# The ends of four down projections written out again: norm scalings left to the scheduler, a second result turned one product later, two products exchanged

## The chip, the cores and the metric

The kernel runs on one core of a Trainium2 chip. The metric is the device time of one execution in microseconds (us). Five engines work side by side, each through its own queue in order: TensorE (PE in the profile, its weight loads PEld), VectorE (DVE), ScalarE (ACT), GpSimd (POOL) and SyncE (SP, which issues transfers). A tile pool hands out buffers in turn; who writes a buffer again waits until its last reader is done.

## What is computed

A trunk of two layers over 512 positions of width 1024. Each layer has a half step with a gated feed-forward, a mixer (banded and dilated attention in layer 0, neighbourhood attention in layer 1), a second half step, and a per-layer input:

```python
def swiglu(x, w_gate, w_up, w_down):
    return (jax.nn.silu(x @ w_gate) * (x @ w_up)) @ w_down
...
    for i in range(DEPTH):
        h = h + 0.5 * swiglu(rmsnorm(h, norm_ffn1[i]), ffn1_w_gate[i], ffn1_w_up[i], ffn1_w_down[i])
        hn = rmsnorm(h, norm_mix[i])
        ...
        h = h + 0.5 * swiglu(rmsnorm(h, norm_ffn2[i]), ffn2_w_gate[i], ffn2_w_up[i], ffn2_w_down[i])
        gate = jax.nn.sigmoid(rmsnorm(h, norm_ple[i]) @ w_ple_gate[i])
        h = h + gate * (p[i] @ w_ple_proj[i])
    return rmsnorm(h, norm_final)
```

The product with `w_down` (2816 x 1024) is made four times: two half steps in each of two layers. These four are the down stages of this text.

## The kernel before

Activations lie as feature chunks: `h` is eight tiles of 128 features x 512 positions (chunks 0 to 7). Every number of a product is split in two parts, `wh` (or `hi`) and `wl` (or `lo`), and a product is three matmuls (hi by hi, hi by lo, lo by hi). `split` (L154, L155) makes the parts: ScalarE copies the first (L154), VectorE subtracts it for the second (L155). Weights land in `wr` (128 x 1024) or `tmp` (128 x 512) tiles; `wh` and `wl` have four buffers each, which are handed out in the order in which the weights are split.

`down` makes the product from seven products of quarters, called "first" to "seventh", each in six steps (step 0 has one chunk of the inner dimension, the others two). A step with two chunks is twelve matmuls of 128 x 512 into two banks. The list `order` (L605 to L608) is the order of all the steps. For each, `product` issues the matmuls (L595), `after` what follows it, and `ahead` the splits for the step four places later and the loads for a step behind that. Within `down`, `put` pins an instruction: it stays in program order on its engine. What is not pinned the scheduler places.

The end of a down stage goes like this. After "sixth" 5 (the last step of "sixth"), ScalarE copies two banks (L601, `c2`), VectorE makes `u3` (L656) and takes it off `c5` (L658): `c5` is one of four results, the right half of the positions of chunks 4 to 7. After "fourth" 5 VectorE makes `c21` (L662), the right half of chunks 0 to 3, whose left half, `c11`, has been ready for long. "third" 0 to 5 give the last result, the left half of chunks 4 to 7.

The results have positions on the partitions, so TensorE turns them back: `turned` (L614) makes transposes of 128 x 128 by the identity `ident`. `second_half(m, ...)` turns two chunks into one bank of `tbank` (tag `tr`, two buffers) and VectorE adds them to `h` (L630). `first_half(m)` turns one whole chunk and VectorE adds it (L620). Behind each sum `norm_split` prepares the chunk for the next stage's products: ScalarE scales it by the norm's gain (L217), VectorE makes the lower part (L218). In the kernel before all of this is pinned:

| after | what is issued |
|---|---|
| "third" 1 | `second_half` of chunks 4 and 5, from `c5` |
| "third" 2 | `second_half` of chunks 6 and 7, from `c5` |
| "fourth" 5 | `c21` |
| "third" 3 | `first_half` of chunks 0 and 1 |
| "third" 4 | `first_half` of chunks 2 and 3 |
| "third" 5 | the left half of chunks 4 to 7 (not pinned, L689 and L690) |

The next stage's first matmuls (L179 to L181 or L785 to L787) take the chunks in the order in which they come and are set between these steps by the scheduler.

Of the kernel before, what the change touches and what calls it, by code (L numbers as in the profile page):

```python
# [56 lines left out]
class Trunk:  # L57
# [92 lines left out]
    def put(self, ins):  # L150
        return self.tc.keep_in_program_order(ins) if self.pinned else ins
# [341 lines left out]
    def down(self, w, a, sums, kept, inner, turn):  # L493

        nc, H = self.nc, T // 2
        l, r = slice(0, H), slice(H, T)
# [101 lines left out]
        def copied(p):  # L598
            out = [self.act() for _ in p]
            for o, x in zip(out, p):  # L600
                put(copy(o, x, AF.Copy))  # L601
            return out
# [2 lines left out]
        order += [("seventh", 0), ("second", 5), ("first", 5), ("fifth", 4), ("seventh", 1), ("sixth", 0), ("seventh", 2),  # L605
                  ("fifth", 5), ("sixth", 1), ("seventh", 3), ("fourth", 0), ("sixth", 2), ("seventh", 4), ("fourth", 1),
                  ("sixth", 3), ("seventh", 5), ("fourth", 2), ("sixth", 4), ("fourth", 3), ("third", 0), ("sixth", 5),
                  ("fourth", 4), ("third", 1), ("third", 2), ("fourth", 5), ("third", 3), ("third", 4), ("third", 5)]  # L608

        hs, M = [], KC // 2  # L610

        def turned(out, x, j):
            for i, y in enumerate(x):
                put(nc.tensor.transpose(out[:, i * P:(i + 1) * P], y[:, j * P:(j + 1) * P], self.ident))  # L614

        def first_half(m):
            p, h = self.tbank(), hs[m]
            turned(p[:, l], c11, m)
            turned(p[:, r], c21, m)
            put(nc.vector.scalar_tensor_tensor(h, p, 0.5, h, op0=ALU.mult, op1=ALU.add))  # L620
            self.h[m] = h
            self.norm_split(m)

        def second_half(m, x, c):
            p = self.tbank()
            for j in range(2):
                turned(p[:, j * H:(j + 1) * H], x, m - M + j)
            for j in range(2):
                h = hs[m + j]
                put(nc.vector.scalar_tensor_tensor(h[:, c], p[:, j * H:(j + 1) * H], 0.5, h[:, c], op0=ALU.mult, op1=ALU.add))  # L630
                self.h[m + j] = h
                self.norm_split(m + j, c)

        def after(kind, s):
            nonlocal rb, rc, c11, c5, c2, u3, c21
            if (kind, s) in (("first", 2), ("fifth", 1)):
                turn(range(2) if kind == "first" else range(2, 4))
                if kind == "fifth":
                    rb = [self.tbank(), self.tbank()]
            elif (kind, s) == ("first", 5):  # L640
                c11 = copied(r1)
                for o, p in zip(c11, r2):
                    put(tt(o, p, o, op=ALU.add))
                rc = [self.bank(), self.obank()]
            elif (kind, s) == ("fifth", 5):
                c5 = copied(r3)
            elif (kind, s) == ("fourth", 0) and inner:
                self.p = inner()
            elif (kind, s) == ("first", 3):
                hs.extend(self.act() for _ in range(KC))  # L650
                for m in range(KC):
                    nc.sync.dma_start(hs[m], kept[m])
            elif (kind, s) == ("sixth", 5):
                c2, u3 = copied(r1), [self.act(), self.act()]
                for i in range(2):
                    put(tt(u3[i], c2[i], rb[i], op=sub))  # L656
                for i in range(2):
                    put(tt(c5[i], c5[i], u3[i], op=sub))  # L658
            elif (kind, s) == ("fourth", 5):
                c21 = [self.act(), self.act()]  # L660
                for i in range(2):
                    put(tt(c21[i], rc[i], u3[i], op=ALU.add))  # L662
            elif kind == "third" and 0 < s < 3:
                second_half(M + 2 * s - 2, c5, r)
            elif kind == "third" and 2 < s < 5:
                first_half(2 * s - 6)
                first_half(2 * s - 5)
# [14 lines left out]
        for i, step in enumerate(order):  # L682
            product(*step)
            after(*step)
            ahead(i + LEAD + 1)
# [4 lines left out]
        for m in range(M, KC, 2):  # L690
            second_half(m, c2, l)
# [935 lines left out]
```

## Time and profile before

| | |
|---|---|
| runs | 2014.23, 2016.39, 2023.58 us (median 2016.39) |
| profiled execution | 2018.9 us, of which its span is 2017.1 us |
| TensorE busy | 1979.8 us, 98% of the span; mean granted clock 0.992 |
| VectorE busy | 1551.3 us, 77% |
| ScalarE busy | 1216.8 us, 60% |
| GpSimd busy | 335.1 us, 17% |
| transfers | 348.24 MB, mean 173 GB/s |

A group of instructions in the profile has its line of the kernel, its engine, the operation and `output<-inputs` by the names of the tiles (`mm`, `sc`, `ob`, `tr` are banks). "Idle before" is the time for which the engine stood still ahead of an instruction, with the instruction that released it. In a row by time the columns are the start, the duration, the engine, the line, the operation, the operands, and how many instructions are merged into the row. A row of stretches has for each engine the busy time and the instructions, then the clock granted to TensorE (1.00 is full speed), the share of the transfer engines and GB/s. The four down stages end near 314 to 347, 953 to 981, 1343 to 1377 and 1918 to 1948 us of the span; the text calls these ends 1 to 4.

### The profile page before, as it was taken

Reading aid. Unit: us, or ns where it says so; the run is one execution under the profiler, and the core shown is the slowest. Engines: PE = TensorE matmul, PEld = TensorE weight load, DVE = VectorE, ACT = ScalarE, POOL = GpSimd, SP = SyncE. Lnnn points to the kernel's source line nnn. Section 1 sums busy time; section 2 is a strip of 40 time slices with the busy share of each in tenths; the row PEclk is TensorE's granted clock in tenths of the full one; section 3 lists DMA queues with packets and bytes.
Section 4 is the critical chain, followed back from the end, with each engine's and each line's share of the span. In section 5 each row is a group of like instructions: output and inputs, shape, how many; then the busy total and the mean of one; then the engine's idle time right before and its main releaser. Section 6 shows DMA issues by size and latency. Waiting matters only on the chain.

```text
span 2017.1 us, 28054 instructions
## 1 busy us (share of the span) xinstructions
PE 1979.8 (98%) x9702; PEld 1648.5 (82%) x9702; DVE 1551.3 (77%) x2716; ACT 1216.8 (60%) x2107; POOL 335.1 (17%) x390
## 2 busy tenths in 40 slices
PE   9999999999999999999999999999999999999998
PEld 7888887879888888887888888888888888888776
DVE  7787888698767667787786777876888767778775
ACT  7665656477645565565566556655766565556553
POOL 1111111341211212011122110111000121111111
PEclk9999999999999999999999999999999999999999
DMA  9877796543426787789468785884343577767951
GB/s 273 197 199 158 188 235 204 138 95 81 96 68 227 169 179 179 176 213 256 143 215 191 175 199 138 216 238 144 104 134 101 180 186 186 171 155 218 255 184 42
DMA packets 152223, 348.24 MB, mean 173 GB/s; under 512 B 26512, under 2 KB 34192, under 8 KB 152080
## 3 DMA queue, kind: packets, MB, share of 16 engines
q1 hardware_dynamic: 112128, 235.23, 35.2%
q0 software_dynamic: 39808, 111.17, 31.0%
q8 instruction: 76, 1.25, 0.3%
q14 instruction: 67, 0.55, 0.1%
q10 hardware_dynamic: 144, 0.04, 0.0%
HBM read 318.06 MB, written 17.27 MB: 166 GB/s over the span
## 4 chain that ended last, share of the span: by engine, by line
PE 73%; DVE 8%; issue 7%; DMA 7%; ACT 3%; POOL 1%; SPq 0%; DVEq 0%; POOLq 0%; ACTq 0%
PE mm L595 6%; PE mm L369 5%; PE mm L370 5%; PE mm L368 5%; PE mm L179 5%; PE mm L181 5%; PE mm L180 5%; PE sc L595 4%; DMA wr<-in_gu_dram 3%; DVE wl L155 3%; PE sc L368 3%; PE sc L370 3%; PE sc L369 3%; PE ob L595 2%; PE tr L595 2%
## 5 line engine op out<-in xcount | busy, mean ns | idle before, releaser
L154 ACT ACTIVATE wh<-wr 128x1024 fp32r<-128x1024 f32 (+1 forms) x428 | 437.6, 1028 | 412.8 <-DMA wr<-in_gu_dram 74.7
L155 DVE TENSOR_TENSOR wl<-wr,wh 128x1024 fp32r<-128x1024 f32 (+1 forms) x428 | 509.4, 1195 | 188.0 <-ACT wh L154 184.3
L368 PE MATMUL mm<-wh,act 128*128 128x512 f32 x640 | 250.7, 392 | 0.0
L370 PE MATMUL mm<-wh,act 128*128 128x512 f32 x640 | 250.6, 392 | 0.0
L369 PE MATMUL mm<-wl,act 128*128 128x512 f32 x640 | 249.5, 390 | 0.4 <-DVE wl L155 0.4
L179 PE MATMUL mm<-act,wh 128*128 128x512 f32 (+1 forms) x472 | 184.9, 393 | 0.3 <-ACT act L154 0.3
L181 PE MATMUL mm<-act,wl 128*128 128x512 f32 (+1 forms) x472 | 184.8, 391 | 0.0
L180 PE MATMUL mm<-act,wh 128*128 128x512 f32 (+1 forms) x472 | 184.7, 391 | 0.0
L154 ACT ACTIVATE wh<-tmp 128x512 fp32r<-128x512 f32 x248 | 144.7, 623 | 61.5 <-PE sc L370 32.7
L595 PE MATMUL mm<-wh,act 128*128 128x512 f32 x528 | 160.5, 398 | 7.0 <-ACT wh L154 7.0
L155 DVE TENSOR_TENSOR wl<-tmp,wh 128x512 fp32r<-128x512 f32 x248 | 160.2, 684 | 0.8 <-ACT wh L154 0.2
L155 DVE TENSOR_TENSOR act<-act,act 128x512 fp32r<-128x512 f32 (+1 forms) x268 | 140.9, 552 | 4.2 <-ACT act L154 4.1
L338 POOL DMA_DIRECT2D wr<-in_gu_dram x80 | 80.2, 1006 | 374.5 <-DVE wl L155 371.2
L369 PEld LDWEIGHTS mm<-wl,act 128*128 128x128 f32 x640 | 120.2, 188 | 25.7 <-DVE wl L155 1.1
L370 PEld LDWEIGHTS mm<-wh,act 128*128 128x128 f32 x640 | 120.1, 188 | 24.2
L368 PEld LDWEIGHTS mm<-wh,act 128*128 128x128 f32 x640 | 120.3, 188 | 23.8
L154 ACT ACTIVATE act<-act 128x512 fp32r<-128x512 f32 (+1 forms) x268 | 125.8, 513 | 16.1 <-DVE act L312 9.5
L368 PE MATMUL sc<-wh,act 128*128 128x512 f32 x320 | 124.6, 389 | 1.1 <-DVE act L292 1.1
L595 PEld LDWEIGHTS mm<-wh,act 128*128 128x128 f32 x528 | 101.1, 192 | 29.2 <-ACT wh L154 8.4
L370 PE MATMUL sc<-wh,act 128*128 128x512 f32 x320 | 124.7, 390 | 0.0
L369 PE MATMUL sc<-wl,act 128*128 128x512 f32 x320 | 124.5, 389 | 0.0
L547 POOL DMA_DIRECT2D wr<-in_dn_dram x72 | 62.5, 882 | 358.6 <-DVE wl L155 355.8
(260 smaller groups left out, 4324.7 us busy)
## 6 DMA issues: line engine op xcount, KB each, us to landing
wr<-in_gu_dram SPq DMA_DIRECT2D x92, 512.0 KB, 5.3
tmp<-in_gu_dram SPq DMA_DIRECT2D x160, 256.0 KB, 3.6
wr<-in_gu_dram POOLq DMA_DIRECT2D x80, 512.0 KB, 7.8
tmp<-in_dn_dram SPq DMA_DIRECT2D x132, 256.0 KB, 6.1
wr<-in_dn_dram POOLq DMA_DIRECT2D x60, 512.0 KB, 7.9
tmp<-in_gu_dram POOLq DMA_DIRECT2D x80, 256.0 KB, 5.9
wr<-in_dn_dram SPq DMA_DIRECT2D x40, 512.0 KB, 5.7
act<-kept SPq DMA_DIRECT2D x56, 256.0 KB, 5.3
```

What stands on the lines that cost most here:

```text
L154: self.put(self.nc.scalar.activation(hi, src, AF.Copy))
L155: self.put((lo_eng or self.nc.vector).tensor_tensor(lo, src, hi.bitcast(F32), op=ALU.subtract))
L179: mm(out, stat[0], mov[0], start=start, stop=False)
L180: mm(out, stat[0], mov[1], start=False, stop=False)
L181: return mm(out, stat[1], mov[0], start=False, stop=stop)
L338: nc.gpsimd.dma_start(raw, q[:, u * UNIT:(u + 1) * UNIT], accum_op=ALU.add)
L368: mm(p, xh, wh, start=start and k == 0, stop=False, skip_group_check=True)
L369: mm(p, xh, wl, start=False, stop=False, skip_group_check=True)
L370: self.last_mm = mm(p, xl, wh, start=False, stop=stop and k == half - 1, skip_group_check=True)
L547: put(nc.gpsimd.dma_start(raw, b[:, u.start * T:u.stop * T], accum_op=ALU.add))
L595: put(nc.tensor.matmul(p, x[k][a][:, c], w[b][:, j * T:(j + 1) * T], start=start and k == a == b == 0, stop=stop and b == 1 and k == u.sto ...
```

## The change

"third" 1 and "fourth" 4 change places in `order`. The second `second_half` on `c5` comes after "fourth" 5, behind `c21`, and takes chunks 6 and 7; the one after "third" 2 takes chunks 4 and 5. `norm_split` is called unpinned at the ends, behind both sums of a `second_half`:

```diff
-                  ("fourth", 4), ("third", 1), ("third", 2), ("fourth", 5), ("third", 3), ("third", 4), ("third", 5)]
+                  ("third", 1), ("fourth", 4), ("third", 2), ("fourth", 5), ("third", 3), ("third", 4), ("third", 5)]
...
+        def floating(f, *x):
+            pinned, self.pinned = self.pinned, False
+            f(*x)
+            self.pinned = pinned
...
-            self.norm_split(m)
+            floating(self.norm_split, m)
...
-                self.norm_split(m + j, c)
+            for j in range(2):
+                floating(self.norm_split, m + j, c)
...
                     put(tt(c21[i], rc[i], u3[i], op=ALU.add))
-            elif kind == "third" and 0 < s < 3:
-                second_half(M + 2 * s - 2, c5, r)
+                second_half(M + 2, c5, r)
+            elif (kind, s) == ("third", 2):
+                second_half(M, c5, r)
```

Seven lines come in ahead of them, so that the later lines have other numbers: L620 becomes L625, L630 L635, L656 L662, L658 L664, L662 L668, L689 L696, L785 L792.

Three places of end 1 show what moves; the other ends move alike. First ScalarE between "sixth" 5 and the copies of `c2`. Before (`wr` is the weight of "sixth" 5 and then of "fourth" 4; `tmp` to `wh_2999` is "third" 1, to `wh_3015` "third" 2; `act` to `act` are the activations of "fourth" 4):

```order
L154 ACTIVATE wh_2950<-wr_2769 128x1024
L154 ACTIVATE act_2971<-act_1881 128x256
L154 ACTIVATE act_2974<-act_1895 128x256
L154 ACTIVATE wh_2977<-wr_2691 128x1024
L154 ACTIVATE act_2981<-act_1881 128x256
L154 ACTIVATE act_2984<-act_1895 128x256
L154 ACTIVATE wh_2999<-tmp_2934 128x512
L154 ACTIVATE wh_2999<-tmp_2935 128x512
L154 ACTIVATE wh_3015<-tmp_2955 128x512
L154 ACTIVATE wh_3015<-tmp_2956 128x512
L601 ACTIVATE act_3037<-mm_2120 128x512
L601 ACTIVATE act_3038<-mm_2121 128x512
```

Now:

```order
L154 ACTIVATE wh_2950<-wr_2769 128x1024
L154 ACTIVATE wh_2971<-tmp_2918 128x512
L154 ACTIVATE wh_2971<-tmp_2919 128x512
L154 ACTIVATE act_2989<-act_1881 128x256
L154 ACTIVATE act_2992<-act_1895 128x256
L154 ACTIVATE wh_2995<-wr_2691 128x1024
L154 ACTIVATE act_2999<-act_1881 128x256
L154 ACTIVATE act_3002<-act_1895 128x256
L154 ACTIVATE wh_3015<-tmp_2955 128x512
L154 ACTIVATE wh_3015<-tmp_2956 128x512
L601 ACTIVATE act_3037<-mm_2120 128x512
L601 ACTIVATE act_3038<-mm_2121 128x512
```

The two splits of "third" 1 have moved ahead of the weight of "fourth" 4 and its activations.

Second, VectorE from the first sums on `c5` to `c21`. Before (L630 are the sums, L218 the lower parts behind the scaling, L155 splits of the weights of "third" 4 and 5):

```order
L630 SCALAR_TENSOR_TENSOR act_2441<-tr_3097,act_2441 128x256
L218 SCALAR_TENSOR_TENSOR act_3104<-act_2441,gain,act_3103 128x256
L630 SCALAR_TENSOR_TENSOR act_2442<-tr_3097,act_2442 128x256
L218 SCALAR_TENSOR_TENSOR act_3109<-act_2442,gain,act_3108 128x256
L155 TENSOR_TENSOR wl_3113<-tmp_3021,wh_3112 128x512
L155 TENSOR_TENSOR wl_3113<-tmp_3022,wh_3112 128x512
L630 SCALAR_TENSOR_TENSOR act_2443<-tr_3130,act_2443 128x256
L218 SCALAR_TENSOR_TENSOR act_3137<-act_2443,gain,act_3136 128x256
L630 SCALAR_TENSOR_TENSOR act_2444<-tr_3130,act_2444 128x256
L218 SCALAR_TENSOR_TENSOR act_3142<-act_2444,gain,act_3141 128x256
L155 TENSOR_TENSOR wl_3146<-tmp_3063,wh_3145 128x512
L155 TENSOR_TENSOR wl_3146<-tmp_3064,wh_3145 128x512
```

Two rows L662 (`c21`) follow. Now, with L635 for the sums and L668 for `c21`:

```order
L155 TENSOR_TENSOR wl_3098<-tmp_3021,wh_3097 128x512
L155 TENSOR_TENSOR wl_3098<-tmp_3022,wh_3097 128x512
L635 SCALAR_TENSOR_TENSOR act_2441<-tr_3115,act_2441 128x256
L635 SCALAR_TENSOR_TENSOR act_2442<-tr_3115,act_2442 128x256
L218 SCALAR_TENSOR_TENSOR act_3123<-act_2441,gain,act_3122 128x256
L218 SCALAR_TENSOR_TENSOR act_3127<-act_2442,gain,act_3126 128x256
L155 TENSOR_TENSOR wl_3131<-tmp_3063,wh_3130 128x512
L155 TENSOR_TENSOR wl_3131<-tmp_3064,wh_3130 128x512
L668 TENSOR_TENSOR act_3148<-mm_2620,act_3041 128x512
L668 TENSOR_TENSOR act_3149<-ob_2621,act_3042 128x512
```

One pair of sums and scalings has gone from ahead of `c21`, the other pair stands behind the splits of "third" 4, and each pair has its two sums ahead of its two scalings.

Third, VectorE from `c21` to the sums of `first_half`. Before (L620 are the sums, `wr` the weights of the next stage):

```order
L662 TENSOR_TENSOR act_3163<-mm_2620,act_3041 128x512
L662 TENSOR_TENSOR act_3164<-ob_2621,act_3042 128x512
L155 TENSOR_TENSOR wl_3321<-wr_3319,wh_3320 128x1024
L620 SCALAR_TENSOR_TENSOR act_2437<-tr_3179,act_2437 128x512
L155 TENSOR_TENSOR wl_3327<-wr_3325,wh_3326 128x1024
L218 SCALAR_TENSOR_TENSOR act_3186<-act_2437,gain,act_3185 128x512
L620 SCALAR_TENSOR_TENSOR act_2438<-tr_3189,act_2438 128x512
L155 TENSOR_TENSOR wl_3383<-wr_3381,wh_3382 128x1024
```

Now, from the row behind `c21` (L625 are the sums of `first_half`):

```order
L635 SCALAR_TENSOR_TENSOR act_2443<-tr_3152,act_2443 128x256
L635 SCALAR_TENSOR_TENSOR act_2444<-tr_3152,act_2444 128x256
L155 TENSOR_TENSOR wl_3321<-wr_3319,wh_3320 128x1024
L218 SCALAR_TENSOR_TENSOR act_3160<-act_2443,gain,act_3159 128x256
L155 TENSOR_TENSOR wl_3327<-wr_3325,wh_3326 128x1024
L218 SCALAR_TENSOR_TENSOR act_3164<-act_2444,gain,act_3163 128x256
L625 SCALAR_TENSOR_TENSOR act_2437<-tr_3179,act_2437 128x512
L155 TENSOR_TENSOR wl_3383<-wr_3381,wh_3382 128x1024
L218 SCALAR_TENSOR_TENSOR act_3186<-act_2437,gain,act_3185 128x512
L625 SCALAR_TENSOR_TENSOR act_2438<-tr_3189,act_2438 128x512
```

The second pair of sums (L635) stands behind `c21`, and its two scalings and a second weight split stand ahead of the first L625.

On TensorE the twelve matmuls of "third" 1 and of "fourth" 4 have changed places, the four transposes for chunks 6 and 7 have moved from behind "third" 2 to behind "fourth" 5, and the scheduler has set four (ends 1 and 3) or eight (ends 2 and 4) more of the next stage's matmuls between "third" 4 and "third" 5.

## The prediction

> **What bounds the kernel now.** I read the page first, then who waits for whom on TensorE, then the instructions in order of time at the end of each down stage, then the chain of waits through the first of these ends.
>
> ```profile
> span 2017.1 us, 28054 instructions
> PE 1979.8 (98%) x9702; PEld 1648.5 (82%) x9702; DVE 1551.3 (77%) x2716; ACT 1216.8 (60%) x2107; POOL 335.1 (17%) x390
> ...
> PE tr L614 <- DVE act L662: 9.6, 7, 3.1
> PE mm L595 <- ACT wh L154: 7.0, 2, 3.6
> PE tr L614 <- DVE act L658: 1.3, 4, 0.4
> ```
>
> TensorE bounds nearly everything, so a change of order can only earn what TensorE loses. Two of its largest waits are transposes (L614) at the ends of the down stages: they wait for L662 (the sums c21) and L658 (c5). The wait on L154 lies elsewhere (in stages two and four, before these ends) and the change does not reach it.
>
> End 1, TensorE, in order of time (start, duration, instructions, idle before and its releaser); the first row begins "sixth" 5, 327.58 "fourth" 5, 337.92 "third" 4, and 346.48 is the first next-stage matmul behind "third" 5:
>
> ```profile
> 314.62 1.98 PE L595 MATMUL mm<-wh,act 128*128 128x512 f32 x8
> ...
> 323.48 0.33 PE L614 MATMUL tr<-ident,act 128*128 128x128 f32 x1 [0.38 <-DVE act L658]
> ...
> 327.58 0.48 PE L595 MATMUL mm<-wh,act 128*128 128x512 f32 x1
> ...
> 333.14 0.38 PE L614 MATMUL tr<-ident,act 128*128 128x128 f32 x2
> 336.61 0.33 PE L614 MATMUL tr<-ident,act 128*128 128x128 f32 x1 [3.09 <-DVE act L662]
> ...
> 337.92 3.49 PE L595 MATMUL sc<-wh,act 128*128 128x512 f32 x8
> ...
> 342.17 0.60 PE L614 MATMUL tr<-ident,act 128*128 128x128 f32 x4
> ...
> 346.48 0.39 PE L179 MATMUL ob<-act,wh 128*128 128x512 f32 x1
> ```
>
> The same places of ends 2, 3 and 4:
>
> ```profile
> 953.74 1.98 PE L595 MATMUL mm<-wh,act 128*128 128x512 f32 x8
> ...
> 965.46 0.48 PE L595 MATMUL mm<-wh,act 128*128 128x512 f32 x1
> ...
> 971.03 0.38 PE L614 MATMUL tr<-ident,act 128*128 128x128 f32 x2
> ...
> 973.70 2.07 PE L595 MATMUL sc<-wh,act 128*128 128x512 f32 x8
> ...
> 980.87 0.39 PE L179 MATMUL mm<-act,wh 128*128 128x512 f32 x1
> ...
> 1343.80 1.98 PE L595 MATMUL mm<-wh,act 128*128 128x512 f32 x8
> ...
> 1367.46 3.76 PE L595 MATMUL sc<-wh,act 128*128 128x512 f32 x8
> ...
> 1376.64 0.39 PE L179 MATMUL ob<-act,wh 128*128 128x512 f32 x1
> ...
> 1918.58 1.98 PE L595 MATMUL mm<-wh,act 128*128 128x512 f32 x8
> ...
> 1935.88 0.38 PE L614 MATMUL tr<-ident,act 128*128 128x128 f32 x2
> ...
> 1939.28 3.25 PE L595 MATMUL sc<-wh,act 128*128 128x512 f32 x8
> ...
> 1947.64 0.39 PE L179 MATMUL mm<-act,wh 128*128 128x512 f32 x1
> ```
>
> All four ends run the same eight products and 24 transposes between those marks, yet take 31.9, 27.1, 32.8 and 29.1 us. End 2 is the yardstick. There "fourth" 5 and "third" 3 take 971.03 - 965.46 = 5.57, so 2.79 a product; the four products and two groups of four transposes before them take 11.72, so 0.28 a group. Its eight transposes after 971.03 take 2.67 instead of 0.56: 2.1 lost. End 1 loses 31.9 - 27.1 + 2.1 = 6.8, end 3 7.8, end 4 4.0. Together 20.7 us can be had here.
>
> The loss is more than idle time. Eight matmuls of "third" 4 take 2.07 in end 2, but 3.49, 3.76 and 3.25 in the others, and the clock row says why:
>
> ```profile
> 338.00:340.00 2.00, 2.00 (x7) 1.61 (x6) 2.00 (x4) 1.08 (x2) 0.58 (x1) 0.50 0.26 49
> ```
>
> The granted clock (third column from the right) was 0.50 right behind the wait. A stretch without products of 2.7 us (end 2) left the clock alone; 3.4 us (end 4) and 4.8 (end 1) did not.
>
> Why c21 is late, VectorE and ScalarE at end 1 (the last row is VectorE at end 2):
>
> ```profile
> 316.24 1.06 ACT L154 ACTIVATE wh<-wr 128x1024 fp32r<-128x1024 f32 x1 [2.70 <-DMA wr<-in_dn_dram]
> ...
> 319.14 2.49 DVE L155 TENSOR_TENSOR wl<-tmp,wh 128x512 fp32r<-128x512 f32 x4
> ...
> 322.74 1.28 DVE L658 TENSOR_TENSOR act<-act,act 128x512 f32<-128x512 f32 x2
> ...
> 327.63 0.42 DVE L630 SCALAR_TENSOR_TENSOR act<-tr,act 128x256 f32<-128x256 f32 x1
> ...
> 328.62 0.48 DVE L218 SCALAR_TENSOR_TENSOR act<-act,gain,act 128x256 fp32r<-128x256 f32 x1 [0.58 <-ACT act L217]
> ...
> 334.66 1.29 DVE L155 TENSOR_TENSOR wl<-tmp,wh 128x512 fp32r<-128x512 f32 x2
> ...
> 335.05 1.99 ACT L154 ACTIVATE wh<-wr 128x1024 fp32r<-128x1024 f32 x2
> ...
> 335.87 0.68 DVE L662 TENSOR_TENSOR act<-mm,act 128x512 f32<-128x512 f32 x1
> ...
> 337.07 1.21 DVE L155 TENSOR_TENSOR wl<-wr,wh 128x1024 fp32r<-128x1024 f32 x1
> ...
> 338.20 0.68 DVE L620 SCALAR_TENSOR_TENSOR act<-tr,act 128x512 f32<-128x512 f32 x1
> ...
> 338.92 0.72 ACT L217 ACTIVATE act<-act,gain 128x512 fp32r<-128x512 f32 x1 [1.88 <-DVE act L620]
> ...
> 339.93 0.74 DVE L218 SCALAR_TENSOR_TENSOR act<-act,gain,act 128x512 fp32r<-128x512 f32 x1
> ...
> 958.71 1.28 DVE L658 TENSOR_TENSOR act<-act,act 128x512 f32<-128x512 f32 x2
> ```
>
> VectorE takes its queue in order. From c5 (324.0) to c21 (337.15) it works almost without a break, save 0.58 at each of four L218 rows, where it waits for ScalarE's scaling of the sum it has just made.
>
> **The change part by part.** No instruction is added or removed, and the sequences on the SP and POOL queues stand as they were, but for one late weight load that moves behind two transfers of h; the exchanged steps issue no accumulating transfer.
>
> *The exchange.* "third" 1 (two 128x512 splits) now precedes "fourth" 4, whose weights wait for a transfer until 316.24. Two of the four splits in the row of 319.14 thus run in that gap: 2 x 0.6 = 1.2 less between 317 and c5, so c5 is done at 322.8. Its transposes now come behind three products, not two: "sixth" 5 ends at 314.62 + 2.79 = 317.4, so they are asked for at 325.8. The waits on L658 go. In ends 2 and 4 c5 is on time already, and this part earns nothing.
>
> *Second result later, scaling set free.* Ahead of c21 there now stand four L155 splits, c21's own two rows, one pair of sums and one pair of scalings instead of two of each, and the two scalings wait for ScalarE once, not four times. From c5 at 322.8: the work of 324.0 to 327.63 is kept (3.6), then a pair of splits 1.2 (334.66 to 335.87), two sums 0.8, two scalings with one wait 1.0, a pair of splits 1.2, c21 1.3: 331.9 instead of 337.15. TensorE ends "third" 3 at 314.62 + 6 x 2.79 + 2 x 0.28 = 331.9. The wait of 3.1 is covered, by nothing to spare, and with it the clock's fall ("third" 4 took 342.17 - 337.92 = 4.25 instead of 2.79: 1.5).
>
> *What is late next.* The second pair of sums now stands behind c21 (+0.8, 332.7) and frees the bank that the second group of transposes needs (332.2): 0.5 lost. "third" 4 starts at 333.0 and ends at 335.8. Between, VectorE has a next-stage split, a scaling, a split and a scaling before the first L625: 1.13 + 0.48 + 1.13 + 0.48 + 0.68 after 332.7 = 336.6, and the third group of transposes waits for the bank it frees: 0.8. Behind it the first next-stage matmuls wait for the scaling (0.72) and then for the split and L218 (1.13 + 0.74): about 0.5 each. Together 2.3 in ends 1 and 3. In ends 2 and 4 VectorE is 1.9 us further ahead of TensorE (c5 done 3.5 behind the end of "sixth" 5, at 959.99 against 956.5; here 5.4), and six next-stage matmuls that need no new scaling stand between: I leave 0.3.
>
> Between "third" 4 and "third" 5 of ends 1 and 3 TensorE then has some 4 us with eight transposes and seven matmuls. From end 2, where 2.7 us with transposes alone did no harm, I take it that the clock holds there. [...]
>
> *Sum.* Ends 1 to 4 earn 6.8 - 2.3, 2.1 - 0.3, 7.8 - 2.3 and 4.0 - 0.3: 15.5 us. The profiled execution took 2018.9 us, so 2003.4; I say 2003.5. It stood 2.5 above the median of the runs (2016.39), which may be one fall of the clock more or less; the change removes those falls, so I do not take the gain from the median (2000.9), but keep that in the range. No row shows the price of a scaling set free: at best it costs nothing further (20.7 in all), at worst it hands c21's delay on to the bank of the third group.
>
> **The rivals.**
> *All of it comes back*, 2018.9 - 20.7 = 1998.2, or 1995.7 from the median: for it speaks that the scheduler set only two scalings before L625; against it the bank waits above.
> *The delay is handed on.* If the clock falls in the thin stretches between "third" 4 and "third" 5, as it did after 336.61, each end loses 1.5 more, and if c21 is 0.5 late as well, four ends lose 8: 2011.5. For it speaks how close 331.9 stands to 331.9; against it end 2 again.
> *Slower: the next stage's weights come late.* VectorE now takes two of its splits before the first L625, where one stood. If their transfers landed w late at each end, all behind would wait w; only from w = (15.5 + 10) / 4 = 6.4 us on would the kernel be slower by 0.5%. Against it: ScalarE split both at 335.05 without a wait.
> *The change doesn't do what it says*: the scalings stand where they did and c21 is no earlier, 2014 to 2018. Against it: the order of instructions.
>
> **How the numbers follow.** The runs before lie 0.5% apart, so 0.5% (10 us) is about what can be told from no change. Chances: the forecast, 2000 to 2007, 0.57; all of it back 0.12; delay handed on, 2007 to 2013, 0.23 (half of it by falls of the clock alone); no effect 0.04; slower 0.04. Faster by over 0.5% (below 2006.3) takes the second and most of the first: 0.67; same 0.29; slower 0.04. The range 1998 to 2011.5 takes in both neighbours but for their outer parts and leaves out less than 0.2.
>
> **What would show it.** In the profile after: the waits of L614 on L668 (c21) under 2 us in all and on L664 (c5) none; the row of eight matmuls of "third" 4 at 2.1 in each end; 346.48 - 314.62 = 31.9 down to about 27.5 with a few more next-stage matmuls inside; new waits of L614 on L635 or L625. Wrong would be: L668 still behind the end of "third" 3 by over 1 us, granted clock 0.5 between "third" 4 and 5, or waits of DVE on transfers of the next stage.

## The result and the profile after

| | before | after |
|---|---|---|
| median of four executions | 2016.43 us | 2002.29 us |
| lowest to highest | 2014.23 to 2023.58 | 1998.39 to 2004.02 |
| profiled execution, its span | 2018.9, 2017.1 us | 2003.01, 2001.2 us |

The ratio is 0.9921, with a 95% interval from 0.9892 to 0.995: 0.8% faster. The sum of the prediction gave 2003.4 for the profiled execution; it took 2003.01. The stretches compared below come from one profiled execution of each kernel.

The busy times of the page after, and the waits of TensorE that answer to those shown of before (engine, line, releaser: us in all, times, longest):

```profile
span 2001.2 us, 28069 instructions
...
PE 1974.6 (99%) x9702; PEld 1644.8 (82%) x9702; DVE 1551.5 (78%) x2716; ACT 1218.5 (61%) x2107; POOL 334.7 (17%) x390
```

```profile
PE mm L595 <- ACT wh L154: 6.3, 2, 3.3
...
PE tr L614 <- DVE act L635: 0.7, 2, 0.4
...
PE ob L180 <- DVE act L218: 0.6, 2, 0.3
...
PE tr L614 <- DVE act L625: 0.4, 2, 0.2
```

The waits for `c21` (9.6 us) and `c5` (1.3) are gone. In their place stand three small ones: for the bank that the second pair of sums frees (L635), for the bank of the first whole chunk (L625), and for a lower part (L218).

End 1 after, TensorE, in order of time: "sixth" 5, the transposes of `c5`, the first group of `first_half`, the second, "third" 4, the third group, next-stage matmuls, "third" 5, and the first row of the next stage's statistic (L235):

```profile
314.68 1.98 PE L595 MATMUL mm<-wh,act 128*128 128x512 f32 x8
...
325.57 0.60 PE L614 MATMUL tr<-ident,act 128*128 128x128 f32 x4
...
331.98 0.60 PE L614 MATMUL tr<-ident,act 128*128 128x128 f32 x4
332.94 0.63 PE L614 MATMUL tr<-ident,act 128*128 128x128 f32 x4 [0.37 <-DVE act L635]
333.33 2.09 PE L595 MATMUL sc<-wh,act 128*128 128x512 f32 x8
...
336.52 0.66 PE L614 MATMUL tr<-ident,act 128*128 128x128 f32 x4 [0.18 <-DVE act L625]
337.27 0.50 PE L179 MATMUL ob<-act,wh 128*128 128x512 f32 x1
...
338.54 0.50 PE L180 MATMUL ob<-act,wh 128*128 128x512 f32 x1 [0.28 <-DVE act L218]
...
339.70 2.10 PE L595 MATMUL sc<-wh,act 128*128 128x512 f32 x8
...
358.76 0.95 PE L235 MATMUL tr<-ones,ssq 128*128 128x1 f32 x8
```

"third" 4 starts at 333.33 instead of 337.92, and its eight matmuls take 2.09 instead of 3.49; in the other three ends they take 2.09, too.

For all comparisons from here on I use one measure: the stretch from the start of "sixth" 5 to that L235 row. TensorE does the same work in it in every kernel (two runs below add fillers): 96 matmuls of products, 32 transposes, and the same next-stage matmuls, wherever the scheduler sets them. These are 72 of 128x512 in ends 2 and 4 (0.227 us apart), but 48 of these and 48 of 128x256 (0.12 apart) in ends 1 and 3, so that ends 1 and 3 have 0.3 us more to do. After, end 1 takes 358.76 - 314.68 = 44.08; before, with the L235 row

```profile
363.38 0.95 PE L235 MATMUL tr<-ones,ssq 128*128 128x1 f32 x8
```

it took 48.76. The four ends before: 48.76, 43.73, 49.76, 45.66, together 187.91; after: 44.08, 42.15, 44.00, 42.15, together 172.38. That is 15.5 of the 15.9 us by which the spans differ: what else differs between the two executions cancels but for 0.4.

VectorE after, end 1: `c5`, the two scalings' lower parts with their one wait, the second row of `c21`, the sums behind it, the first L625:

```profile
321.63 1.29 DVE L664 TENSOR_TENSOR act<-act,act 128x512 f32<-128x512 f32 x2
...
328.72 0.89 DVE L218 SCALAR_TENSOR_TENSOR act<-act,gain,act 128x256 fp32r<-128x256 f32 x2 [0.25 <-ACT act L217]
...
331.45 0.68 DVE L668 TENSOR_TENSOR act<-ob,act 128x512 f32<-128x512 f32 x1
332.05 0.75 DVE L635 SCALAR_TENSOR_TENSOR act<-tr,act 128x256 f32<-128x256 f32 x2
...
335.77 0.69 DVE L625 SCALAR_TENSOR_TENSOR act<-tr,act 128x512 f32<-128x512 f32 x1
```

`c21` is done at 332.13, when its transposes are due. The stretches of two microseconds between "third" 4 and "third" 5 (busy time and instructions of PE, PEld, DVE, ACT and POOL, then the granted clock):

```profile
336.00:338.00 2.00, 1.72 (x10) 1.03 (x8) 1.87 (x3) 1.74 (x3) 0.58 (x1) 1.00 0.85 242
338.00:340.00 2.00, 1.73 (x11) 1.31 (x10) 1.21 (x3) 0.88 (x2) 0.56 (x1) 1.00 0.85 311
```

The clock stays at 1.00, and TensorE is busy for 86% of this place, which the prediction had called thin.

### The profile page after: what moved, and what is told of

It reads as the page before. It is cut to its first block, busy times and chain, and to the rows that moved or that the text cites. A ratio compares the mean times of both kernels' runs of the same rounds, so it can differ in the third digit from the quotient of the medians.

```text
span 2001.2 us, 28069 instructions
## 1 busy us (share of the span) xinstructions
PE 1974.6 (99%) x9702; PEld 1644.8 (82%) x9702; DVE 1551.5 (78%) x2716; ACT 1218.5 (61%) x2107; POOL 334.7 (17%) x390
## 4 chain that ended last, share of the span: by engine, by line
PE 60%; issue 6%; DVE 6%; DMA 5%; ACT 2%; POOL 1%; SPq 0%; DVEq 0%; POOLq 0%; ACTq 0%
PE mm L179 5%; PE mm L181 5%; PE mm L180 5%; PE mm L595 5%; PE mm L369 4%; PE mm L370 4%; PE mm L368 4%; PE sc L595 3%; DMA wr<-in_gu_dram 3%; PE sc L370 2%; PE sc L369 2%; PE sc L368 2%; DVE wl L155 2%; PE ob L595 2%; PE sc L181 1%
## 5 line engine op out<-in xcount | busy, mean ns | idle before, releaser
L155 DVE TENSOR_TENSOR wl<-wr,wh 128x1024 fp32r<-128x1024 f32 (+1 forms) x428 | 509.8, 1195 | 176.5 <-ACT wh L154 168.0
L369 PE MATMUL mm<-wl,act 128*128 128x512 f32 x640 | 249.5, 390 | 0.1
L180 PE MATMUL mm<-act,wh 128*128 128x512 f32 (+1 forms) x472 | 183.9, 390 | 0.0
L155 DVE TENSOR_TENSOR wl<-tmp,wh 128x512 fp32r<-128x512 f32 x248 | 160.5, 684 | 2.9 <-ACT wh L154 2.5
L155 DVE TENSOR_TENSOR act<-act,act 128x512 fp32r<-128x512 f32 (+1 forms) x268 | 141.2, 554 | 3.9 <-ACT act L154 3.7
L369 PEld LDWEIGHTS mm<-wl,act 128*128 128x128 f32 x640 | 120.2, 188 | 24.9 <-DVE wl L155 0.7
L368 PEld LDWEIGHTS mm<-wh,act 128*128 128x128 f32 x640 | 120.3, 188 | 23.8
L369 PE MATMUL sc<-wl,act 128*128 128x512 f32 x320 | 124.6, 389 | 0.0
```

The costliest lines, as they stand in the source:

```text
L155: self.put((lo_eng or self.nc.vector).tensor_tensor(lo, src, hi.bitcast(F32), op=ALU.subtract))
L180: mm(out, stat[0], mov[1], start=False, stop=False)
L368: mm(p, xh, wh, start=start and k == 0, stop=False, skip_group_check=True)
L369: mm(p, xh, wl, start=False, stop=False, skip_group_check=True)
```

## Experiments

The theory: what counts is how late VectorE is with `c21` and with the sums behind it, and its waits for ScalarE ahead of the lower parts (L218) are the largest part of that; a fall of the clock needs one of TensorE's waits. The rivals: all three parts of the change are needed together; or the place of the second result carries it; or the falls have nothing to do with the waits.

All combinations of the three parts were run. The table also has for each end how long after the start of "sixth" 5 `c5` was done, whose order of instructions no part but the exchange changes.

| kernel | ends 1 to 4, us | sum | `c5` done after |
|---|---|---|---|
| before | 48.76 43.73 49.76 45.66 | 187.91 | 9.40 6.25 9.50 6.55 |
| second result later | 48.13 43.13 49.17 43.44 | 183.87 | 9.40 6.71 9.33 6.74 |
| exchange | 46.52 43.28 46.02 44.85 | 180.67 | 8.20 5.82 8.23 7.37 |
| exchange, later | 45.32 43.14 46.98 43.39 | 178.83 | 8.16 5.82 8.26 5.81 |
| scalings free | 44.73 44.45 45.57 43.28 | 178.03 | 8.59 8.61 9.41 7.42 |
| exchange, free | 46.62 42.29 44.07 43.48 | 176.46 | 8.18 5.81 7.29 6.99 |
| later, free | 44.32 42.15 45.05 42.15 | 173.67 | 8.52 6.74 9.25 6.24 |
| after (all three) | 44.08 42.15 44.00 42.15 | 172.38 | 8.24 5.81 8.17 5.81 |

### Scalings free

```diff
-            self.norm_split(m)
+            floating(self.norm_split, m)
...
-                self.norm_split(m + j, c)
+            for j in range(2):
+                floating(self.norm_split, m + j, c)
```

> Only the scalings are set free (both sums first, norm_split unpinned); order of steps and place of the second result as before. Measure: the sum over the four ends of the stretch from the start of "sixth" 5 to the first L235 row (187.91 us before, 172.38 after). Theory: the scaling waits on VectorE carry most. A pair of sums and scalings takes some 1.9 us instead of 2.96, two pairs stand ahead of c21, so c21 is 2.1 us earlier; its wait in ends 1 and 3 falls from 3.4 to about 1.2 us, in ends 2 and 4 to nothing; the stretch without products falls under 2.7 us, so the eight matmuls of "third" 4 take 2.1 us in all ends. Gains about 3.7, 1.5, 4.3 and 3.2: 12.7 of the 15.5 us, 2003.5 to 2005 against 2016.4. L664 (c5) keeps its 1.3 us of waits. Rival A (all three parts are needed together): under 6 us. Rival B (moving the second result carries it): under 3 us.

Measured: 2007.42 us against 2019.64, ratio 0.9943 (0.9927 to 0.9959); sum 178.03, a gain of 9.9 us. End 3, TensorE: the wait for `c21` and "third" 4 behind it:

```profile
1357.07 0.33 PE L614 MATMUL tr<-ident,act 128*128 128x128 f32 x1 [1.08 <-DVE act L668]
...
1358.18 2.07 PE L595 MATMUL sc<-wh,act 128*128 128x512 f32 x8
```

Ends 1 and 3 gained 4.0 and 4.2, near what was expected (3.7 and 4.3): the wait fell from 3.1 to 1.1, and no end had a fall of the clock. In end 1 `c5` also came 0.8 earlier than before, so that only end 3 is a fair measure. Rivals A and B are out. The sum missed the expected 12.7, and the median the expected 2003.5 to 2005 (the profiled execution took 2003.8).

VectorE at end 3, a pair of sums and its lower parts:

```profile
1350.07 0.75 DVE L635 SCALAR_TENSOR_TENSOR act<-tr,act 128x256 f32<-128x256 f32 x2
1351.06 0.89 DVE L218 SCALAR_TENSOR_TENSOR act<-act,gain,act 128x256 fp32r<-128x256 f32 x2 [0.25 <-ACT act L217]
```

The pair waits 0.25 once, where before each L218 waited 0.58. The edit has two halves, and the trace tells them apart here: from `c5` to behind "third" 5, in all four ends, VectorE's order differs from before only in that each second sum stands ahead of the first scaling, and ScalarE's does not differ. The scheduler did nothing with its freedom there, so this gain is that of the order of the sums. What the freedom is worth behind `c21` in the kernel after, no run separates.

End 2 lost 0.7, where a gain of 1.5 had been expected. The reason is a weight. ScalarE at end 2, the weight of "fourth" 4 in this run, and in the kernel before:

```profile
946.87 1.06 ACT L154 ACTIVATE wh<-wr 128x1024 fp32r<-128x1024 f32 x1 [3.52 <-DMA wr<-in_dn_dram]
```

```profile
952.20 1.06 ACT L154 ACTIVATE wh<-wr 128x1024 fp32r<-128x1024 f32 x1 [3.30 <-PE ob L595]
```

Here the split waits for the transfer and starts 0.81 us behind "sixth" 5. Before it waited for the buffer that TensorE frees, 1.54 us ahead of "sixth" 5, and the weight was there. So `c5` was done after 8.6 us instead of 6.25. Such lateness comes without any edit as well: up to end 1 the kernels without the exchange have the same order of instructions, yet `c5` comes after 8.5 to 9.4 us there. Over all 14 traces (before, after and the twelve runs) it comes after more than 7 us in each of the 28 ends 1 and 3, but in 7 of the 28 ends 2 and 4 only. So ends 2 and 4 are mostly ahead, as the prediction had read them, but not in every execution; the text calls an end with more than 7 late. A sum over ends mixes an edit with this luck, and like ends must be compared. Where `c5` came after 9.25 us or more, before took 48.76 and 49.76, free scalings 45.57, later and free 45.05.

### Second result later

```diff
-            elif kind == "third" and 0 < s < 3:
-                second_half(M + 2 * s - 2, c5, r)
+                second_half(M + 2, c5, r)
+            elif (kind, s) == ("third", 2):
+                second_half(M, c5, r)
```

> Only the second result is moved behind "fourth" 5; scalings stay pinned, no exchange. Theory: c21 comes 3 us earlier, but behind it stands a pinned sum, a next-stage split, a scaling with its wait for ScalarE, and only then the second sum, which frees the bank for the second group of transposes; so "third" 4 starts at about 337 as before, now behind L630, and the clock still falls in ends 1, 3 and 4. Gain 1 to 4 us of 15.5, sum 184 to 187. Rival B (c21's place carries the gain): waits on L662 and the clock's fall go, 10 us or more.

Measured: ratio 0.998 (0.9969 to 0.9992), sum 183.87: 4.0 us, of which 2.2 in end 4, where the clock held this time. End 1, TensorE, and VectorE behind `c21`:

```profile
335.79 0.63 PE L614 MATMUL tr<-ident,act 128*128 128x128 f32 x4 [1.96 <-DVE act L630]
336.17 3.50 PE L595 MATMUL sc<-wh,act 128*128 128x512 f32 x8
```

```profile
333.70 1.21 DVE L155 TENSOR_TENSOR wl<-wr,wh 128x1024 fp32r<-128x1024 f32 x1
334.83 0.47 DVE L218 SCALAR_TENSOR_TENSOR act<-act,gain,act 128x256 fp32r<-128x256 f32 x1
335.23 0.41 DVE L630 SCALAR_TENSOR_TENSOR act<-tr,act 128x256 f32<-128x256 f32 x1
```

Of the wait for `c21` 1.3 us were left in ends 1 and 3, and 1.96 came up at the bank: a next-stage split and a pinned scaling stand between the two sums that free it. The clock falls in ends 1 and 3 as before; in end 4 it was expected to fall and held. In ends 1 and 3 the second result's new place earns 0.6 us by itself.

### Exchange

```diff
-                   ("fourth", 4), ("third", 1), ("third", 2), ...
+                   ("third", 1), ("fourth", 4), ("third", 2), ...
```

> Only "third" 1 and "fourth" 4 are exchanged; the first result then follows the first of the two products. Theory: c5 is ready at about 322.8 in end 1 (324.0 before) but asked for at 320.2, so a wait of 2.6 us on L658 appears in ends 1 and 3, of 0.7 in ends 2 and 4. It moves lost time forward: c21 is 1.2 us earlier and "third" 3 ends 2.7 later, so its wait falls to about 0.6 and the clock does not fall there. Gain about 6 us (2.7, 0, 2.7, 1), or 3 if the clock falls behind the new wait. Rival A (all three parts are needed): 0 or a loss.

Measured: ratio 0.9955 (0.9938 to 0.9971), sum 180.67, a gain of 7.2. End 1, the transposes of `c5`, and the clock two microseconds on:

```profile
322.05 0.33 PE L614 MATMUL tr<-ident,act 128*128 128x128 f32 x1 [2.06 <-DVE act L658]
```

```profile
324.00:326.00 2.00, 2.00 (x6) 1.59 (x5) 1.42 (x5) 0.51 (x1) 0.00 (x0) 0.50 0.22 61
```

The wait on L658 is there (2.1 in ends 1 and 3), and `c5` comes 1.2 earlier than before, as the prediction's step had it. In end 1 the clock fell behind the new wait, in end 3 behind an equal one (2.09) it did not. That the exchange alone gained goes with `c5` being 1.2 us earlier in ends 1 and 3, and with one fall of the clock instead of three; of the falls one is chance, as ends 1 and 3 show.

### Pairs of two parts

> The exchange and the second result later, scalings pinned as before: after without its floating scalings. Theory: the waits on c5 go, c21 is in time, but the pinned scaling between the two sums behind c21 holds the bank; "third" 4 starts at about 335.9 in end 1 (337.9 before, 333.3 after), the stretch without products stays near 4 us, and the clock still falls in ends 1 and 3. Gain about 4.5 us of 15.5 (2.2, 0, 2.2, 0), sum about 183. Rival B (place of the second result and the exchange carry it): 12 us or more.

Measured: ratio 0.9947 (0.9933 to 0.9962), a gain of 9.1. TensorE of end 1 and then of end 3:

```profile
335.44 0.63 PE L614 MATMUL tr<-ident,act 128*128 128x128 f32 x4 [1.95 <-DVE act L630]
335.83 2.07 PE L595 MATMUL sc<-wh,act 128*128 128x512 f32 x8
...
1360.10 0.63 PE L614 MATMUL tr<-ident,act 128*128 128x128 f32 x4 [1.96 <-DVE act L630]
1360.48 3.23 PE L595 MATMUL sc<-wh,act 128*128 128x512 f32 x8
```

"third" 4 started where expected (335.8), but two ends that are alike to 0.1 us part here (2.39 and 2.48 us idle ahead of "third" 4): in end 1 the clock held, in end 3 it fell. The expectation, which let both fall, was too low by 1.2 us in end 1 and by 2.9 in ends 2 and 4, most of it in end 4, where the clock held.

> The exchange and the floating scalings, but the second result stays behind "third" 2: after without the later second result. Theory: the first result follows the first of the exchanged products, so c5 is asked for too early as in the exchange alone (2.1 us of wait where c5 comes 8.2 us behind the start of "sixth" 5, under 1.3 elsewhere), while c21 is in time (19.5 us behind that start where the exchange alone had 21.5). Without a fall of the clock the stretch is about 45.3 us where c5 is late and 42.5 where it is not, with 1.5 more where the clock falls behind the new wait: sum over the ends 175 to 178, 10 to 13 us of 15.5. Rival (with the scalings free the second result's place is worth nothing): sum 172.5, as after.

Measured in one execution: 2006.37 us, sum 176.46, within the range. The first waits for `c5` were 2.0, 0.2, 1.1 and 0.8 us, the clock fell once (end 1). The second result's new place is needed because `c5` has to be asked for later.

> The second result later and the scalings free, no exchange. Theory: "fourth" 4 comes first and its weight is late, so c5 is done 9.4 us behind the start of "sixth" 5 where the transfer is late (8.2 in after) and c21 1.2 us later than in after (18.6 against 17.4); "third" 4 then starts at about 19.8 instead of 18.6 in these ends. In ends where the transfer is in time there is no difference to after. Two late ends: sum 174.5 to 176 (172.4 after), each late end more adds 1.2 us. Rival (the exchange is worth nothing once the scalings are free): sum 172.5.

Measured in one execution: 2004.44 us, sum 173.67, just under the range, since in end 1 the transfer was less late than assumed (`c5` after 8.5). End 3, with `c5` after 9.25, took 45.05 against 44.00 after. So with the other two parts made the exchange is worth 1 us in a late end and nothing in the others.

### Work put into the wait

The kernel before, with matmuls of 128x256 or transposes between the `c11` and the `c21` transposes of chunk 0:

```diff
             turned(p[:, l], c11, m)
+            if m == 0:
+                for _ in range(18):
+                    put(nc.tensor.matmul(p[:, r], x4[K2 - 1][0][:, :P], x4[K2 - 1][0], start=True, stop=True, ...))
```

> The kernel before with 18 more matmuls of 128x256 on TensorE between the c11 and the c21 transposes of the first chunk; the c21 transposes overwrite what they write. Some 2 us of work is put into the wait for c21, nothing else is moved by hand. Theory: the clock falls because TensorE is idle too long; with 2 us of the wait filled, the stretch without products is under 3 us in every end, the eight matmuls of "third" 4 take 2.1 us everywhere (3.49, 2.07, 3.76, 3.25 before), and although work is added the ends get shorter where the clock fell before: 1.5 to 2.5 us less in ends 1 and 3, and where c21 is late by less than 2 us the surplus of filler is lost instead (up to 0.9). Rival (the fall has another cause than the gap): "third" 4 stays at 3.2 to 3.8 in some ends, no end is shorter.

> As the run with products in the wait, but with 22 transposes of 128x128 (0.09 us each, 2 us in all) in their place. If any work on TensorE keeps the clock, "third" 4 takes 2.1 us in all four ends, as with the products. If only products count, the stretch without products is as long as before or longer, and the clock falls in ends 1 and 3 at least (3.2 to 3.8 us for the eight matmuls).

End 1 with products, then with transposes:

```profile
333.74 2.40 PE L621 MATMUL tr<-act 128*128 128x256 f32 x18
...
338.19 2.08 PE L595 MATMUL sc<-wh,act 128*128 128x512 f32 x8
```

```profile
332.92 0.38 PE L614 MATMUL tr<-ident,act 128*128 128x128 f32 x2
333.14 2.56 PE L621 MATMUL tr<-ident,act 128*128 128x128 f32 x22
...
337.49 2.09 PE L595 MATMUL sc<-wh,act 128*128 128x512 f32 x8
```

In all eight ends the eight matmuls of "third" 4 took 2.07 to 2.09, although `c21` was as late as ever (22.5 us after "sixth" 5 in ends 1 and 3 with products, 22.53 and 22.63 before). With products, ends 1 and 3 took 47.58 and 47.59 instead of 48.76 and 49.76: 2 us of useless work made them 1.2 and 2.2 us shorter. That the falls come from TensorE's standing still is shown: eight ends without a fall here, three falls in four before. Transposes serve as well as products: 4.6 us without a product (332.92 to 337.49 in end 1) did no harm in four of four ends, where 4.8 us (333.14 to 337.92) and 5.0 with the wait unfilled lost the clock in ends 1 and 3 of before. As times the two kernels are no gain (2020.89 and 2023.29 us, one execution each, 2017.15 for before). With transposes the ends are 3.9 us longer in sum: a new wait of 1.0 us an end came behind "third" 4, for the bank that the first sum of `first_half` frees. With products the ends are 2.3 us shorter in sum (185.63), but the stretch between ends 3 and 4 took 3.9 us more than before (528.97 instead of 525.02): TensorE waited for splits of weights (L369, 3.1 us in the whole run against 0.4 before) and, ahead of end 4, 1.2 for ScalarE, which it did not in the profiled execution of before. That this is chance is not shown; the run with the second result later took 2.5 us more than before between ends 2 and 3. In those two runs more ends were late, too (`c5` after 8.1 to 9.4 us in three and in four of them).

### The delay put back

The kernel after, with four subtractions on VectorE ahead of `c21`:

```diff
                 c21 = [self.act(), self.act()]
+                for _ in range(4):
+                    put(tt(c21[0], u3[0], u3[1], op=sub))
```

> The kernel after with four more subtractions of 128x512 (0.64 us each, 2.56 in all) on VectorE ahead of c21 in each end; they write c21 and are overwritten. Theory: c21 is just in time in ends 1 and 3 and has some 1.5 us to spare in ends 2 and 4, and the bank behind it hangs on it, so nearly all of the delay shows: "third" 4 starts at about 21.2 in ends 1 and 3 (18.6 after) and 19.6 in ends 2 and 4 (18.1), L668 and L635 are waited for again, and in ends 1 and 3 the clock may fall (1.2 us more each). Sum 180 to 183 (172.4 after). Rival (VectorE has slack there, the gain came from elsewhere): sum under 176.

Measured in one execution: 2017.81 us, sum 190.5, so all of the gain is lost and 2.6 us more. The delay was larger than meant; VectorE at end 1 ahead of `c21` (the subtractions are L668 here):

```profile
329.85 1.22 DVE L155 TENSOR_TENSOR wl<-wr,wh 128x1024 fp32r<-128x1024 f32 x1
...
332.31 1.22 DVE L155 TENSOR_TENSOR wl<-wr,wh 128x1024 fp32r<-128x1024 f32 x1
```

The scheduler set two next-stage splits between the subtractions, so `c21` came 4.2 to 4.9 us later instead of 2.56, "third" 4 at 23.2, 22.2, 23.8 and 22.9 us after "sixth" 5 instead of 18.1 to 18.7, and the clock fell in three ends. The size is missed for that reason. That lateness of VectorE at `c21`, and of the sums behind it, brings back the whole loss is shown. In ends 1 and 3 there was no slack; in end 2 "third" 4 started 4.1 us later for a `c21` 4.9 later, so some 0.9 was to spare.

### What is left in ends 1 and 3

```diff
-        def halved(raw):
+        def halved(raw, lo_eng=None):
...
-                self.split(x, hi[:, c], lo[:, c])
+                self.split(x, hi[:, c], lo[:, c], lo_eng)
...
-                w, x = halved(more.pop((kind, s))), x4
+                w, x = halved(more.pop((kind, s)), nc.gpsimd if s > 3 else None), x4
```

> The kernel after with one thing more: the lower parts of the weights of "third" 4 and "third" 5 (four tiles of 128x512 in each end) are made by GpSimd, which has nothing to do there, instead of VectorE. Theory: what is left in ends 1 and 3 (44.0 us against 42.15 in ends 2 and 4) is VectorE being late for the sums that free banks (L635, L625) and for L218; 2.4 us less on its queue ends these waits. Ends 1 and 3 come to 42.2 to 42.6, the sum from 172.4 to about 169.3, the time to 1998 to 2000. Rival: GpSimd takes longer for a tile than VectorE and slows VectorE beside it, or the rest is not VectorE's: sum 172 or more, time as after or above.

Measured: 2000.24 us, ratio 0.9914 (0.9898 to 0.9931); ends 43.22, 42.15, 43.29, 42.13, sum 170.79. The waits on L635 and L625 are gone, that on L218 stayed; half of the 3 us expected came. Some of the rest could not come, since ends 1 and 3 have 0.3 us more to do than the 42.15 they were measured against. GpSimd, then VectorE, at end 1:

```profile
325.02 6.64 POOL L155 TENSOR_TENSOR wl<-tmp,wh 128x512 fp32r<-128x512 f32 x4 [10.33 <-ACT wh L154]
```

```profile
327.29 1.96 DVE L218 SCALAR_TENSOR_TENSOR act<-act,gain,act 128x256 fp32r<-128x256 f32 x2 [0.24 <-ACT act L217]
...
331.03 1.71 DVE L155 TENSOR_TENSOR wl<-wr,wh 128x1024 fp32r<-128x1024 f32 x1
```

The four tiles took GpSimd 6.64 us here (in end 2 two of them took 2.55), and beside it the pair of L218 took 1.96 instead of 0.89 and the split 1.71 instead of 1.22: of the 2.4 us taken off VectorE 1.6 came back there.

```diff
             self.h[m] = h
-            floating(self.norm_split, m)
+            if m % 2:
+                for j in range(2):
+                    floating(self.norm_split, m - 1 + j)
```

> The kernel after with one thing more: first_half too has both sums (L625) of a pair ahead of its two scalings. Theory: in after the fourth group of transposes waits for a bank that the second L625 frees, and that stands behind a next-stage split and an L218 that waits for ScalarE; with both sums first it comes at about 337.1 instead of 338.9 in end 1, no next-stage matmuls stand between "third" 4 and "third" 5, and "third" 5 starts 0.8 to 1 us earlier for equal work. Ends 1 and 3 from 44.0 to 43.1, sum about 170.6, time about 2000.5. Rival: the next stage's first matmuls wait for the later scalings instead: sum 172.4 or more.

Measured: 2000.30 us, ratio 0.9905 (0.9891 to 0.9919); ends 42.75, 42.07, 43.19, 42.11, sum 170.12. End 1: the third and the fourth group together, and "third" 5 behind them:

```profile
335.84 1.25 PE L614 MATMUL tr<-ident,act 128*128 128x128 f32 x8 [0.20 <-DVE act L625]
336.85 2.09 PE L595 MATMUL sc<-wh,act 128*128 128x512 f32 x8
```

As expected: in end 3, as late as in after (`c5` after 8.15), it took 0.8 us less, and no other end took longer, so nothing was lost behind it (in end 1 `c5` was 0.5 earlier than in after, which helped). The rival is out.

> Both: the lower parts of the weights of "third" 4 and 5 on GpSimd, and both sums ahead of the scalings in first_half. Theory: with VectorE early (L625 at 334.6 in end 1) the second sum comes at 335.2 instead of 336.7, the transposes of the fourth group no longer wait, and ends 1 and 3 (43.2 with GpSimd alone) reach the 42.2 of ends 2 and 4. Sum 168.6 to 169.2, time about 1998 (2000.2 with GpSimd alone, 2002.3 after). Rival: the wait goes over to the first next-stage matmuls, and the sum stays at 170.8.

Measured: 1999.65 us, ratio 0.99 (0.9884 to 0.9916); ends 43.32, 41.94, 43.06, 42.70, sum 171.02. The theory missed; the rival's sum came, by another wait. TensorE behind "third" 5 of end 1, and VectorE ahead of `c21`:

```profile
341.23 0.33 PE L614 MATMUL tr<-ident,act 128*128 128x128 f32 x1 [0.55 <-DVE act L698]
```

```profile
327.17 3.01 DVE L218 SCALAR_TENSOR_TENSOR act<-act,gain,act 128x256 fp32r<-128x256 f32 x2 [0.25 <-ACT act L217]
```

The pair of L218 took 2.1 us longer beside GpSimd (3.01 instead of 0.89), and in the late ends (three of four here) the last results (L698) came 0.55 late. The three extensions have medians of 1999.65 to 2000.30 against 2002.29 after, and the intervals of their ratios to before overlap with that of after: that any of them is faster than after stays open by time. By the stretches, sums ahead of scalings in `first_half` too is the simplest step on.

## Why the prediction was right, and where it was not

Gains by end, predicted 4.5, 1.8, 5.5 and 3.7, measured 4.7, 1.6, 5.8 and 3.5: 15.5 as a sum both times. The mechanism came as predicted, but for the clock and the sizes of two terms. That the sums agree so closely is in part luck: they hang on which ends were late in two single executions, and on a clock whose falls the runs show to be partly chance.

- *The exchange.* `c5` was due at 322.8 and came at 322.92. That ends 2 and 4 earn nothing from it holds with the other parts made (42.15 with it and without); that `c5` is on time there held in both executions, and fails in 7 of 28 such ends.
- *`c21`.* Due at 331.9, done at 332.13; no wait was left. The term rested on the scalings' waits for ScalarE going from four to one (0.58 each before, 0.25 after), and the runs show that this is the part that carries most: alone it earned 4.2 in end 3, where `c5` was as late as before, the second result's place alone 0.6, and all three together 5.8. The prediction's heading puts this down to the scaling set free; what did it where the trace can tell is the order of both sums first, which its sum counts as "two scalings with one wait".
- *What is late next.* 2.3 in ends 1 and 3 was predicted against 0.3 in the others, so 2.0 between them. 44.08 - 42.15 = 1.9 was measured, but 0.3 of that is the next stage's own work, so 1.6. The parts in end 1, by the starts in end 2: behind L635 0.5 predicted, "third" 4 started 0.56 later (18.65 against 18.09 behind "sixth" 5); the third group 0.8 predicted, 0.36 more (21.84 against 20.92); what stands behind it 1.0 predicted, some 0.7 left over, of which L180's wait for L218 is 0.28. So the places were right, and the third group and what follows were sized too high.
- *The clock.* The outcome was right and the reason wrong. The prediction took from ends 2 and 4 that the length of a stretch without products decides, near 3 us. The runs refute it: in two ends alike to 0.1 us the clock held and fell, and with transposes 4.6 us without a product held. The place between "third" 4 and "third" 5, which the prediction took for thin, had TensorE busy for 86%; that this is why the clock held there fits, but no run tested it.
- *The rivals.* Nothing was handed on by the clock or by late weights, and the change did what it says. "All of it comes back" would have been a sum of 187.9 - 20.7 = 167.2; it is 172.4. One execution after took 1998.39, that rival's time, but only the profiled one shows its ends.
- *Base of the sum.* Taken from the profiled execution's own 2018.9, the sum gave 2003.4 for 2003.01 measured. From the median it would have given 2000.9 for a median of 2002.29. Four executions after lie 5.6 us apart, so that the first came within 0.4 is luck.

## What to carry to other kernels

An in-order engine that makes a value, hands it to another engine and then waits for the answer pays that round trip each time (here 0.58 us ahead of each of four L218, and 0.25 once for a pair with both sums first): issue all the makers of a group first and their followers behind them. Moving a result later helped little here (0.6 us an end) while other work stood between the two sums that free its bank. When similar places in one trace differ, look first for a transfer that came late in some of them, and compare like places; a tendency (here ends 1 and 3) shows only over several executions.

## What was not expected of the hardware

*How the clock falls.* Length of idle time did not decide it. Rows of 12 of the 14 traces show TensorE wholly still 19 times for 2.28 to 3.82 us ahead of a product whose weight was not split yet. In three of them the eight matmuls behind it took 2.11 us (waits of 2.42, 3.44 and 3.54 us), in the other 16 from 2.54 to 3.78. Two of these are the wait of 2.28 us at 1893 us of the run with the exchange and the later result, and that of 3.54 us at the same place (1904 us) of the run with products in the wait:

```profile
1893.01 3.33 PE L595 MATMUL mm<-wh,act 128*128 128x512 f32 x8 [2.28 <-ACT wh L154]
```

```profile
1904.16 2.11 PE L595 MATMUL mm<-wh,act 128*128 128x512 f32 x8 [3.54 <-ACT wh L154]
```

```profile
1894.00:1896.00 2.00, 2.00 (x6) 1.61 (x5) 1.42 (x3) 0.41 (x1) 0.87 (x1) 0.50 1.06 412
```

The shorter wait lost the clock (0.50, eight matmuls in 3.33 us), the longer kept it (1.00, 2.11 us). What decides it is not shown. With 2.56 us of transposes of 128x128 in the wait for `c21` the clock held in four of four ends, where the unfilled wait lost it in three of four.

*GpSimd beside VectorE.* Some of VectorE's instructions took longer while GpSimd subtracted (L218 pairs of 1.96 and 3.01 us instead of 0.89), others did not (both `c21` rows stayed at 0.68). `c21` reads one of its inputs from a bank, L218 none; that this is what sets them apart no run tested. How the two engines' rows overlap in detail is not to be read here, since GpSimd's spans are rough.
